# A decoder layer on one core: the correction pass of the attention scores made 128 rows high, GpSimd's start put behind the loads of x, and the last output block done in two halves

## The chip, the core and the metric

The kernel runs on one core of a Trainium2 chip. Its engines are TensorE (PE in the profile, with its weight loads in a row of their own, PEld), VectorE (DVE), ScalarE (ACT), GpSimd (POOL) and SyncE (SP), which issues transfers. The metric is the device time of one execution in microseconds (us), and a lower one is better.

## The reference

One decoder layer over 512 tokens of width 1024, all in float32. Eight heads do causal attention with a forget gate (a running sum of log gates is added to the logits), eight do causal attention over three dilated windows with a penalty by distance, and both are followed by an output projection. Then a PEER feed-forward picks 16 experts for each of 8 heads and each token out of 16384 and sums them.

```python
xn = rms_norm(h, norm1_g[layer])
proj = xn @ w_in[layer]
...
fox_out = fox_attention(fq, fk, fv, log_f)
dil_out = dilated_attention(dq, dk, dv)
mixed = jnp.concatenate([merge_heads(fox_out), merge_heads(dil_out)], axis=-1)
h = h + mixed @ w_out[layer]
xn2 = rms_norm(h, norm2_g[layer])
h = h + peer_ffn(xn2, peer_wq[layer], peer_subkeys[layer], peer_u[layer], peer_v[layer])
return rms_norm(h, normf_g)
```

## The kernel before, in words

Nearly every product is float32 done by splitting: a number is held as a high part (`hi`, rounded to the type that TensorE reads fast) and a low part (`lo`, what is left), and `mm3` (lines 147 to 153) sums three products hi·hi, hi·lo and lo·hi. ScalarE makes the high part, VectorE the low one.

**Start (lines 248 to 293).** SyncE issues the four blocks of x (128 tokens each), then the weights. ScalarE issues the unit matrix and two small vectors. GpSimd clears `cpart` and issues six loads of constants: `sel`, `maskb`, `iota16`, `mult`, `ndist`, `iota`. The sums of squares of x are taken by ScalarE (blocks 0 and 2, line 277) and by VectorE (blocks 1 and 3, line 278). `normed` (lines 126 to 145) turns a pair of sums into a scaled unit matrix `diag` and transposes x through TensorE with it; ScalarE (line 142) and VectorE (line 143) take the result out of PSUM. Only then do the projections begin, and from there on TensorE has work without a break.

**Attention (lines 323 to 436).** There are four groups `g` of four heads; groups 0 and 1 are the forget-gate heads, 2 and 3 the dilated ones. `project(g)` makes for each head the queries `qs` and keys `kT` as 128-row tiles: `kT` holds the high part of the key in its own 64 rows and the low part in the other 64, `qs` the high part of the query in both halves. `ql` holds the low part of the query, two heads in one tile, each in its 64 rows. `scores` (line 363) does for each head and each block of 128 queries

```python
own = slice(e * HD, (e + 1) * HD)
nc.tensor.matmul(s[:, :n], qs[:, h, i * P:n], kT[:, h, :n], start=True, stop=False)
nc.tensor.matmul(s[:, :n], ql[own, pr, i * P:n], kT[own, h, :n], start=False, stop=(g >= 2))
```

The first (line 373) contracts over 128 rows, the second (line 374, here called the correction pass) over 64. Both stream n = 128, 256, 384 or 512 columns. In groups 0 and 1 two short bfloat16 passes follow (lines 378 and 379: gate sums and mask). Then come the softmax on VectorE and ScalarE (lines 380 to 394), the transposes of the weights p on TensorE (`trans`, line 401), their copy by ScalarE (line 403) and the product with the values (line 424), of which each writes 64 of 128 rows. `attend` runs these as a pipeline of pairs of heads: 32 pairs in all, and a pair's transposes are issued one step after its scores. The score tile `s` in PSUM has 2 buffers, p has 5. `merge` interleaves `attend(g)` with `project(g + 1)`, and a scheduler then fixes the order of the instructions of each engine.

**The rest.** Output projection and second norm (lines 452 to 472), the choice of the experts (lines 556 to 725), and the dense stage (lines 757 to 797), in which each pair of 128 experts gets its products by lines 152 and 792. The tile `oacc[b][d]` sums the output of token block b and column half d. After the loop the last block's 24 matmuls, which alternate between the halves d = 0 and d = 1, end TensorE's work. The tail (lines 800 to 824) adds each block to the residual (line 810), sums squares (lines 812 and 814), and scales (line 821).

Of the kernel before, what the change touches and what calls it, by code (L numbers as in the profile page):

```python
# [71 lines left out]
def tile_kernel(ctx: ExitStack, tc: tile.TileContext, x, w_in, w_f, b_f, w_out, wq, skT, u, v, uT, g1, g2, g2r, gfr,  # L72
# [53 lines left out]
    def normed(pp, src, b0, ss, g, name, then=None):  # L126

        diag = small.tile([P, 2, P], F32, name="diag")
# [103 lines left out]
    with ExitStack() as st:  # L232
# [6 lines left out]
        mult = abf.tile([P, TB, P], F32, name="mult")  # L239
# [3 lines left out]
        qss = [qkv.tile([P, 4, T], F32R, name=f"qs{i}") for i in range(2)]  # L243
        qls = [qkv.tile([P, 2, T], F32R, name=f"ql{i}") for i in range(2)]
# [3 lines left out]
        with ExitStack() as s1:  # L248
# [18 lines left out]
            with tc.manual_schedule(engines={ET.Pool}):  # L267
                nc.gpsimd.memset(cpart, 0.0)
                for t, src in ((sel, csel), (maskb, cmask), (iota16, ciota16)):
                    nc.gpsimd.dma_start(t, src)  # L270
                nc.gpsimd.dma_start(mult, cmult)
                nc.gpsimd.dma_start(ndist, cdist)
                nc.gpsimd.dma_start(iota, ciota)
            nc.vector.tensor_copy(identb, ident)
            ss = small.tile([P, TB], F32, name="n1ss")
            for b0 in range(0, TB, 2):
                nc.scalar.activation(junk[0], xs[b0 // 2][:, 0, :], AF.Square, accum_out=ss[:, b0:b0 + 1])
                nc.vector.tensor_tensor_reduce(out=junk[1], in0=xs[b0 // 2][:, 1, :], in1=xs[b0 // 2][:, 1, :], scale=1.0, scalar=0.0,
                                               op0=ALU.mult, op1=ALU.add, accum_out=ss[:, b0 + 1:b0 + 2])
                _, _, norm1 = normed(xt, xs[b0 // 2], b0, ss[:, b0:b0 + 2], g1c, "n1", feed.start if b0 else None)  # L280
# [42 lines left out]
            def project(g):  # L323
                qs, ql, kT, vs = qss[g % 2], qls[g % 2], kTs[g % 2], vss[g % 2]
                for kind in range(3):
                    w = feed.get()
                    for n in range(2):
                        ps = pj.tile([P, T], F32, name="pj")
                        if kind < 2:
                            mm3(ps, cols(w, n), XT)  # L330
                            for e in range(2):
                                h = 2 * n + e
                                own, oth = slice(e * HD, (e + 1) * HD), slice((1 - e) * HD, (2 - e) * HD)
                                if kind == 0:
                                    sc = 1.0 / math.sqrt(HD) / (1.0 if g < 2 else SLOPES[4 * (g - 2) + h])
                                    hi = qs[own, h, :]
                                    nc.scalar.activation(hi, ps[own], AF.Copy, scale=sc)
                                    nc.scalar.activation(qs[oth, h, :], ps[own], AF.Copy, scale=sc)
# [24 lines left out]
        def scores(g, i, pr):  # L363
            qs, ql, kT = qss[g % 2], qls[g % 2], kTs[g % 2]
# [4 lines left out]
            for e in range(2):  # L369
                h = 2 * pr + e  # L370
                s = pS.tile([P, T], F32, name="s")
                own = slice(e * HD, (e + 1) * HD)
# [79 lines left out]
        for c in range(D // WC):  # L452
# [4 lines left out]
            for b in range(0, TB, 2):  # L457
# [9 lines left out]
                if c == D // WC - 1:  # L467
                    ss = small.tile([P, 2], F32, name="n2ss")
                    nc.vector.tensor_reduce(ss, sq[:, b:b + 2, :], axis=AX.X, op=ALU.add)
                    rs, norm2, _ = normed(xt, hb, b, ss, g2t, "n2")  # L470
# [256 lines left out]
    with ExitStack() as st:  # L727
# [29 lines left out]
        def dense():  # L757
            load_v(0)
            load_v(1)
            for i in range(NPAIR + 1):  # L760
# [18 lines left out]
                if i > 0:  # L779
# [5 lines left out]
                    for j, (n, c, b) in enumerate(order):  # L785
# [4 lines left out]
                        for w, m, s0, s1 in ((ah, vh, first_, False), (al, vh, False, False), (ah, vl, False, last_)):  # L790
                            for d in range(2):
# [108 lines left out]
```

## Time and profile before

| | |
|---|---|
| median of 3 runs | 1567.56 us (1567.28 to 1568.92) |
| the profiled execution | 1568.9 us |
| its span, first instruction to last | 1567.0 us |
| mean granted clock of TensorE | 0.992 of full |
| busy share of the span: TensorE, its weight loads, VectorE, ScalarE, GpSimd | 97%, 86%, 77%, 41%, 24% |
| chain that ended last: TensorE, VectorE, ScalarE, transfers | 82%, 12%, 3%, 2% |

The profiled execution is 1.3 us above the median, and 1.9 us of its time lie outside the span. Busy shares are of the whole span. Matmuls are pipelined: a matmul's own duration overlaps the next one's, so the distance from one start to the next says what a matmul costs. "Idle before" and the waits name the engine and the tile whose work ended last before an instruction could start; "issue" is time in which nothing that the profile shows was waited for. Where the heights of the two operands matter, the profile writes them before the shape: 64\*128 is a pass over 64 rows with 128 columns of weights.

### The profile page before, as it was taken

The numbers are of one execution on the slowest core, as the hardware profiler recorded it, in microseconds if no ns is written. First come the engines' busy times: TensorE is split into PE (matmuls) and PEld (weight loads), VectorE is DVE, ScalarE is ACT, GpSimd is POOL, SyncE is SP. The second block draws the span as 40 slices with busy tenths as digits, with TensorE's granted clock in tenths as the row PEclk, the third lists the DMA queues.
The fourth block names the chain that finished last, engine by engine and source line by source line (L and its number), as shares of the span: only waits on it lengthen the run. The fifth ranks groups of instructions, "written<-read, shape, count | busy, mean of one in ns | idle before, by whom it ended". The sixth has DMA issues, their size and how long they took to land.

```text
span 1567.0 us, 22166 instructions
## 1 busy us (share of the span) xinstructions
PE 1524.7 (97%) x8637; PEld 1344.4 (86%) x8641; DVE 1205.0 (77%) x2251; ACT 649.0 (41%) x804; POOL 377.9 (24%) x269
## 2 busy tenths in 40 slices
PE   6999999989999999999999999999999999999997
PEld 6777777978899898989888889888898888988886
DVE  6554476439999999996877787787778787877886
ACT  6354454332233766767333333333333333333332
POOL 1000000000002010001345435444444343444440
PEclk9999999999999999999999999999999999999999
DMA  5211110422237585868999898989999999998984
GB/s 198 82 54 55 55 54 29 175 81 81 82 138 265 219 296 198 303 225 326 373 365 349 327 325 316 364 312 338 331 324 333 328 338 325 324 322 324 345 273 161
DMA packets 139289, 380.39 MB, mean 243 GB/s; under 512 B 9392, under 2 KB 58672, under 8 KB 134448
## 3 DMA queue, kind: packets, MB, share of 16 engines
q1 hardware_dynamic: 95968, 228.87, 41.4%
q0 software_dynamic: 37600, 135.09, 23.3%
q10 hardware_dynamic: 5616, 15.02, 2.5%
q8 instruction: 68, 1.11, 0.3%
q14 instruction: 37, 0.30, 0.1%
HBM read 338.90 MB, written 40.37 MB: 242 GB/s over the span
## 4 chain that ended last, share of the span: by engine, by line
PE 82%; DVE 12%; ACT 3%; DMA 2%; issue 1%; SPq 0%; DVEq 0%; ACTq 0%
PE pj L152 39%; PE oa L792 33%; DVE wlo L124 3%; PE pg L711 2%; PE o L424 2%; PE s L374 1%; PE t L401 1%; PE xt L140 1%; ACT whi L123 1%; PE s L373 1%; ACT gs L701 1%; PE psc L576 1%; DVE og L689 1%; DMA gt<-Gd 1%; DVE eq L651 1%
## 5 line engine op out<-in xcount | busy, mean ns | idle before, releaser
L152 PE MATMUL pj<-xh,whi 128*128 128x384 f32 (+1 forms) x1288 | 453.0, 352 | 5.9 <-ACT hs L523 3.6
L152 PE MATMUL pj<-xh,wlo 128*128 128x384 f32 (+1 forms) x1288 | 451.7, 351 | 1.5 <-DVE wlo L124 1.5
L152 PE MATMUL pj<-xl,whi 128*128 128x384 f32 (+1 forms) x1288 | 450.1, 349 | 0.0
L493 POOL DMA_INDIRECT row<-in_u_dram,eidx x128 | 190.0, 1485 | 691.7 <-DVE hid L502 276.4
L123 ACT ACTIVATE whi<-wraw 128x2048 fp32r<-128x2048 f32 (+1 forms) x89 | 169.8, 1908 | 264.0 <-PE pj L152 254.8
L152 PEld LDWEIGHTS pj<-xh,whi 128*128 128x128 f32 x1288 | 243.4, 189 | 20.2 <-issue 4.7
L152 PEld LDWEIGHTS pj<-xh,wlo 128*128 128x128 f32 x1288 | 243.2, 189 | 12.6 <-DVE wlo L124 2.1
L152 PEld LDWEIGHTS pj<-xl,whi 128*128 128x128 f32 x1288 | 243.3, 189 | 11.2
L124 DVE TENSOR_TENSOR wlo<-wraw,whi 128x2048 fp32r<-128x2048 f32 (+1 forms) x89 | 202.3, 2274 | 55.6 <-ACT whi L123 55.6
L493 POOL DMA_INDIRECT row<-in_v_dram,eidx x128 | 182.2, 1423 | 242.3 <-DVE acc L509 211.3
L792 PE MATMUL oa<-vh,ah 128*128 128x512 f32 x768 | 237.3, 390 | 1.3 <-ACT ah L123 1.3
L792 PE MATMUL oa<-vh,al 128*128 128x512 f32 x768 | 237.5, 390 | 0.3 <-DVE al L124 0.3
L792 PE MATMUL oa<-vl,ah 128*128 128x512 f32 x768 | 237.6, 391 | 0.0
L123 ACT ACTIVATE vh<-vr 128x2048 fp32r<-128x2048 f32 x64 | 122.9, 1920 | 242.9 <-PE oa L792 213.3
L509 DVE SCALAR_TENSOR_TENSOR acc<-row,a,acc 128x1024 f32<-128x1024 f32 x128 | 164.2, 1283 | 20.9 <-DMA row<-in_v_dram,eidx 18.3
L792 PEld LDWEIGHTS oa<-vh,al 128*128 128x128 f32 x768 | 144.3, 188 | 31.3 <-DVE al L124 0.7
L792 PEld LDWEIGHTS oa<-vl,ah 128*128 128x128 f32 x768 | 144.6, 188 | 30.5
L502 DVE CUSTOM_DVE_ANT_0 row<-row,xn 128x1024 f32<-128x1024 f32 x128 | 152.1, 1220 | 22.3 <-DMA row<-in_u_dram,eidx 22.3
L792 PEld LDWEIGHTS oa<-vh,ah 128*128 128x128 f32 x768 | 143.9, 188 | 29.3 <-ACT ah L123 1.6
L124 DVE TENSOR_TENSOR vl<-vr,vh 128x2048 fp32r<-128x2048 f32 x64 | 146.2, 2285 | 0.0
L772 DVE TENSOR_TENSOR ga<-gt,ga 128x384 f32<-128x384 f32 x128 | 67.9, 553 | 65.4 <-ACT ga L523 57.4
L124 DVE TENSOR_TENSOR al<-ga,ah 128x768 fp32r<-128x768 f32 x64 | 61.3, 958 | 62.0 <-ACT ah L123 62.0
(207 smaller groups left out, 1639.7 us busy)
## 6 DMA issues: line engine op xcount, KB each, us to landing
wraw<-in_uT_dram SPq DMA_DIRECT2D x64, 1024.0 KB
vr<-in_v_dram SPq DMA_DIRECT2D x64, 1024.0 KB
Gd<-gs SPq DMA_DIRECT2D x12, 2048.0 KB
gt<-Gd SPq DMA_DIRECT2D x32, 768.0 KB
wraw<-in_w_in_dram SPq DMA_DIRECT2D x12, 1024.0 KB
Hd<-hs ACTq DMA_DIRECT2D x28, 384.0 KB
ga<-Hd SPq DMA_DIRECT2D x28, 384.0 KB
wraw<-in_wq_dram SPq DMA_DIRECT2D x8, 1024.0 KB
```

What stands on the lines that cost most here:

```text
L123: nc.scalar.activation(hi, src, AF.Copy)
L124: nc.vector.tensor_sub(lo, src, hi.bitcast(F32))
L140: nc.tensor.matmul(pt[:, kc % 2, e, :], src[:, e, kc * P:(kc + 1) * P], diag[:, e, :], start=True, stop=True)
L152: nc.tensor.matmul(ps, a, c, start=(i == 0), stop=(i == 3 * n - 1))
L373: nc.tensor.matmul(s[:, :n], qs[:, h, i * P:n], kT[:, h, :n], start=True, stop=False)
L424: nc.tensor.matmul(o[e * HD:(e + 1) * HD, pr, :], vs[:, j, h * HD:(h + 1) * HD], pts[e][:, j * P:(j + 1) * P], start=(j == 0), stop=(j == i))
L493: nc.gpsimd.indirect_dma_start(out=rows[n], out_offset=None, in_=tab, in_offset=bass.IndirectOffsetOnAxis(ap=eidx[:, k:k + 1], axis=0))
L502: nc.vector.tensor_tensor_reduce(out=t, in0=t, in1=xn0, scale=1.0, scalar=0.0, op0=ALU.mult, op1=ALU.add, accum_out=hid0[:, k:k + 1])
L509: nc.vector.scalar_tensor_tensor(acc, t, a0[:, k:k + 1], acc, op0=ALU.mult, op1=ALU.add)
L711: nc.tensor.matmul(pg[:, tt, :], w[2][:, t4 + tt, :], w[3][:, n, t4 + tt, :], start=(n == 0), stop=(n == 1))
L772: nc.vector.tensor_mul(a, gt[:, :, c, :], a)
L792: nc.tensor.matmul(oacc[b][d], w[:, c, sl], m[:, c, d * 512:(d + 1) * 512], start=s0, stop=s1)
```

## The change

There are three parts.

1. **Correction pass.** `ql` is gone. `qs` gets a second plane: `qs[:, 1, h, :]` holds the low part of the query in the head's own 64 rows, and zeros in the other 64. Both score passes now contract over 128 rows. To make room, `mult` becomes bfloat16, p has 4 buffers instead of 5, and `diag` moves into pools of the two norms, which end early. The zeros are written once, by four fills of GpSimd.
2. **GpSimd's start.** Its first fill waits for VectorE's sum of squares of the last block of x (line 270 of the new kernel), and with it the six loads of constants and the four new fills, which stand behind it.
3. **Last block.** The last block's 24 matmuls do all twelve of half d = 0 first, then all twelve of d = 1.

```diff
-    def normed(pp, src, b0, ss, g, name, then=None):
+    def normed(pp, sp, src, b0, ss, g, name, then=None):
-        diag = small.tile([P, 2, P], F32, name="diag")
+        diag = sp.tile([P, 2, P], F32, name="diag", bufs=2)
...
-        mult = abf.tile([P, TB, P], F32, name="mult")
+        mult = abf.tile([P, TB, P], BF16, name="mult")
-        qss = [qkv.tile([P, 4, T], F32R, name=f"qs{i}") for i in range(2)]
-        qls = [qkv.tile([P, 2, T], F32R, name=f"ql{i}") for i in range(2)]
+        qss = [qkv.tile([P, 2, 4, T], F32R, name=f"qs{i}") for i in range(2)]
...
-            with tc.manual_schedule(engines={ET.Pool}):
-                nc.gpsimd.memset(cpart, 0.0)
-                for t, src in ((sel, csel), (maskb, cmask), (iota16, ciota16)):
-                    nc.gpsimd.dma_start(t, src)
-                nc.gpsimd.dma_start(mult, cmult)
-                nc.gpsimd.dma_start(ndist, cdist)
-                nc.gpsimd.dma_start(iota, ciota)
...
+            with tc.manual_schedule(engines={ET.Pool}):
+                first = nc.gpsimd.memset(cpart, 0.0)
+                tc.add_manual_dep(first.ins, sums.ins.name, mybir.DependencyInfo(mybir.DependencyClass.Sync, mybir.DependencyReason.DATA),
+                                  reason="the loads of x come first")
+                for t, src in ((sel, csel), (maskb, cmask), (iota16, ciota16), (mult, cmult), (ndist, cdist), (iota, ciota)):
+                    nc.gpsimd.dma_start(t, src)
+                for i in range(2):
+                    z = qss[i][:, 1].rearrange("p (a b) t -> p a b t", b=2)
+                    nc.gpsimd.memset(z[0:HD, :, 1, :].bitcast(F32), 0.0)
+                    nc.gpsimd.memset(z[HD:P, :, 0, :].bitcast(F32), 0.0)
...
-                                    nc.vector.scalar_tensor_tensor(ql[own, n, :], ps[own], sc, hi.bitcast(F32), op0=ALU.mult, op1=ALU.subtract)
+                                    nc.vector.scalar_tensor_tensor(qs[own, 1, h, :], ps[own], sc, hi.bitcast(F32), op0=ALU.mult, op1=ALU.subtract)
...
-                nc.tensor.matmul(s[:, :n], qs[:, h, i * P:n], kT[:, h, :n], start=True, stop=False)
-                nc.tensor.matmul(s[:, :n], ql[own, pr, i * P:n], kT[own, h, :n], start=False, stop=(g >= 2))
+                for part in range(2):
+                    nc.tensor.matmul(s[:, :n], qs[:, part, h, i * P:n], kT[:, h, :n], start=(part == 0), stop=(part == 1 and g >= 2))
-                p = wk.tile([P, T], F32, name="p", bufs=5)
+                p = wk.tile([P, T], F32, name="p", bufs=4)
...
-                    for j, (n, c, b) in enumerate(order):
+                    halves = [(e, (0, 1)) for e in order if i < NPAIR or e[2] < TB - 2]
+                    halves += [(e, (d,)) for d in range(2) for e in order if i == NPAIR and e[2] == TB - 2]
+                    for j, ((n, c, b), ds) in enumerate(halves):
...
-                            for d in range(2):
+                            for d in ds:
```

GpSimd's queue from its first fill, before (names are tiles; `in_...` are inputs; the row's end is the shape):

```order
L268 MEMSET cpart 128x512
L270 DMA sel<-in_csel_dram 128x1024
L270 DMA maskb<-in_cmask_dram 128x128
L270 DMA iota_112<-in_ciota_dram 128x16
L271 DMA mult<-in_cmult_dram 128x512
L272 DMA ndist<-in_cdist_dram 128x512
L273 DMA iota<-in_ciota_dram 128x128
L308 MEMSET ln 128x512
L482 MEMSET acc 128x1024
```

The same queue in the changed kernel, in which the first of these rows waits for VectorE:

```order
L276 MEMSET cpart 128x512
L280 DMA sel<-in_csel_dram 128x1024
L280 DMA maskb<-in_cmask_dram 128x128
L280 DMA iota_112<-in_ciota_dram 128x16
L280 DMA mult<-in_cmult_dram 128x512
L280 DMA ndist<-in_cdist_dram 128x512
L280 DMA iota<-in_ciota_dram 128x128
L283 MEMSET qs_128 64x2x512
L284 MEMSET qs_128 64x2x512
L283 MEMSET qs_129 64x2x512
L284 MEMSET qs_129 64x2x512
L312 MEMSET ln 128x512
```

The six loads keep their order and stand behind the wait; the four fills of `qs` come after them and before the fill of `ln`, which the gates need.

VectorE's queue at the end of the program, before. `oa_7574` and `oa_7575` are the last block's halves d = 0 and d = 1, L810 adds them, L814 squares, L109 to L114 make the scale, and the L821 pair scales the block before the last:

```order
L810 TENSOR_TENSOR row<-row,oa_7574 128x512
L810 TENSOR_TENSOR row<-row,oa_7575 128x512
L109 RECIPROCAL n3r<-n3s 128x1
L814 ISA vh,n3ss<-row 128x512
L814 ISA n3ss 128x1
L111 SCALAR_TENSOR_TENSOR n3t<-n3r 128x1
L817 TENSOR_TENSOR n3sm<-n3ss 128x1
L112 TENSOR_TENSOR n3t<-n3t,n3v 128x1
L105 TENSOR_SCALAR n3v<-n3sm 128x1
L114 SCALAR_TENSOR_TENSOR n3q<-n3t,n3r 128x1
L821 SCALAR_TENSOR_TENSOR row<-row,n3q,vr 128x512 x2
L109 RECIPROCAL n3r<-n3s 128x1
```

The same place in the changed kernel; here the halves are `oa_7576` and `oa_7577`, and L816, L820, L823 and L827 stand for L810, L814, L817 and L821. First the five rows from the add of d = 0 on, in which the L827 pair scales the second block:

```order
L816 TENSOR_TENSOR row<-row,oa_7576 128x512
L114 SCALAR_TENSOR_TENSOR n3q<-n3t,n3r 128x1
L823 TENSOR_TENSOR n3sm<-n3ss 128x1
L827 SCALAR_TENSOR_TENSOR row<-row,n3q,vr 128x512 x2
L105 TENSOR_SCALAR n3v<-n3sm 128x1
```

and the rows right behind them, up to the pair that scales the block before the last:

```order
L816 TENSOR_TENSOR row<-row,oa_7577 128x512
L820 ISA vh,n3ss<-row 128x512
L820 ISA n3ss 128x1
L109 RECIPROCAL n3r<-n3s 128x1
L823 TENSOR_TENSOR n3sm<-n3ss 128x1
L111 SCALAR_TENSOR_TENSOR n3t<-n3r 128x1
L105 TENSOR_SCALAR n3v<-n3sm 128x1
L112 TENSOR_TENSOR n3t<-n3t,n3v 128x1
L114 SCALAR_TENSOR_TENSOR n3q<-n3t,n3r 128x1
L109 RECIPROCAL n3r<-n3s 128x1
L827 SCALAR_TENSOR_TENSOR row<-row,n3q,vr 128x512 x2
```

The add of d = 0 has moved up by five rows, and the first step of the last block's scale (the second L109) now stands ahead of the L827 pair, where it stood behind it. On TensorE, VectorE and ScalarE every other instruction stands where it stood, the attention included: a correction pass stands in each place where one stood.

## Rows read from the trace of the kernel before

**Rows 1.** The page, section 1: busy us, share, instructions of each engine.

```profile
PE 1524.7 (97%) x8637; PEld 1344.4 (86%) x8641; DVE 1205.0 (77%) x2251; ACT 649.0 (41%) x804; POOL 377.9 (24%) x269
```

**Rows 2.** Busy times of the attention's stretch: PE, PEld, DVE, ACT, POOL; clock, DMA.

```profile
57.00:275.00 218.00, 215.12 (x1368) 166.21 (x1371) 114.09 (x307) 106.18 (x230) 0.95 (x1) 0.99 0.15 54
```

**Rows 3.** Waits, 57 to 275 us: who <- what: us in total, times, longest.

```profile
PEld s L374 <- issue: 9.6, 42, 0.3
...
PEld L378 <- issue: 3.7, 17, 0.3
...
DVE p L384 <- PE t L401: 0.6, 1, 0.6
```

**Rows 4.** The correction pass by its line: duration ns min/median/max, first and last start.

```profile
L374 PE MATMUL s<-kT,ql x64: 322/410/503, 57.0 to 265.4; 64*128 64x128 f32 x16, 64*128 64x256 f32 x16, 64*128 64x384 f32 x16, 64*128 64x512 f32 x16
```

**Rows 5.** Timeline of TensorE, 256 columns: start us, us, instruction.

```profile
248.65 0.28 PE L373 MATMUL s<-kT,qs 128*128 128x256 f32 x1
248.86 0.38 PE L374 MATMUL s<-kT,ql 64*128 64x256 f32 x1
...
249.40 0.28 PE L152 MATMUL pj<-wlo,mixh 128*128 128x256 f32 x1
249.51 0.28 PE L373 MATMUL s<-kT,qs 128*128 128x256 f32 x1
```

**Rows 6.** The same view, 512 columns.

```profile
259.47 0.39 PE L373 MATMUL s<-kT,qs 128*128 128x512 f32 x1
...
260.44 0.28 PE L152 MATMUL pj<-wlo,mixh 128*128 128x256 f32 x1
```

**Rows 7.** The same view, 128 columns.

```profile
130.28 0.22 PE L373 MATMUL s<-kT,qs 128*128 128x128 f32 x1
...
130.68 0.23 PE L378 MATMUL s<-cpart,sel 128*128 128x128 bf16 x1
```

**Rows 8.** TensorE's timeline at its one long wait in the attention.

```profile
72.08 0.33 PE L373 MATMUL s<-kT,qs 128*128 128x128 f32 x1 [1.35 <-ACT p L381]
```

**Rows 9.** Timeline: last multiplication of p and first transpose behind it, first pair, last-but-one pair.

```profile
72.61 0.48 DVE L394 TENSOR_SCALAR p<-p,rz 128x128 f32<-128x128 f32 x2
...
73.30 0.39 PE L401 MATMUL t<-ident,p 128*128 128x128 f32 x2
...
267.94 0.88 DVE L394 TENSOR_SCALAR p<-p,rz 128x512 f32<-128x512 f32 x2
...
268.58 0.63 PE L401 MATMUL t<-ident,p 128*128 128x128 f32 x4
```

**Rows 10.** Busy times as in rows 2, after the wait of rows 8; clock 0.58.

```profile
73.00:77.00 4.00, 4.00 (x14) 3.16 (x15) 1.93 (x7) 1.74 (x7) 0.00 (x0) 0.58 0.01 4
```

**Rows 11.** VectorE's timeline at the start: first `diag`, last block of x.

```profile
8.47 0.42 DVE L131 TENSOR_TENSOR diag<-ident,n1q 128x256 f32<-128x256 f32 x1
10.89 1.22 DVE L278 CUSTOM_DVE_ANT_0 junk<-xs 128x1024 bf16<-128x1024 f32 x1 [1.99 <-DMA xs<-in_x_dram]
```

**Rows 12.** SyncE's DMA queue in 4 to 5 us, then 5 to 8 us: packets, MB, share.

```profile
q1 hardware_dynamic: 105, 0.41, 98.7%
...
q1 hardware_dynamic: 159, 0.57, 51.2%
```

**Rows 13.** Timeline: a fill of GpSimd beside a VectorE instruction with two inputs.

```profile
40.37 2.28 DVE L124 TENSOR_TENSOR wlo<-wraw,whi 128x2048 fp32r<-128x2048 f32 x1
...
40.58 0.53 POOL L308 MEMSET ln<- 128x512 f32 x1 [35.84 <-ACT qs L338]
```

**Rows 14.** The page, section 5: the same VectorE instruction in all its places.

```profile
L124 DVE TENSOR_TENSOR wlo<-wraw,whi 128x2048 fp32r<-128x2048 f32 (+1 forms) x89 | 202.3, 2274 | 55.6 <-ACT whi L123 55.6
```

**Rows 15.** VectorE's timeline in the tail.

```profile
1557.69 1.29 DVE L810 TENSOR_TENSOR row<-row,oa 128x512 f32<-128x512 f32 x2 [1.07 <-PE oa L792]
...
1560.27 1.41 DVE L821 SCALAR_TENSOR_TENSOR row<-row,n3q,vr 128x512 f32<-128x512 f32 x2
...
1562.38 0.75 DVE L821 SCALAR_TENSOR_TENSOR row<-row,n3q,vr 128x512 f32<-128x512 f32 x1
```

More of the change, by code (lines that the diff above doesn't have):

```diff
@@ L277, in tile_kernel @@
                 nc.scalar.activation(junk[0], xs[b0 // 2][:, 0, :], AF.Square, accum_out=ss[:, b0:b0 + 1])
-                nc.vector.tensor_tensor_reduce(out=junk[1], in0=xs[b0 // 2][:, 1, :], in1=xs[b0 // 2][:, 1, :], scale=1.0, scalar=0.0,
+                sums = nc.vector.tensor_tensor_reduce(out=junk[1], in0=xs[b0 // 2][:, 1, :], in1=xs[b0 // 2][:, 1, :], scale=1.0, scalar=0.0,
                                                op0=ALU.mult, op1=ALU.add, accum_out=ss[:, b0 + 1:b0 + 2])
-                _, _, norm1 = normed(xt, xs[b0 // 2], b0, ss[:, b0:b0 + 2], g1c, "n1", feed.start if b0 else None)
+                _, _, norm1 = normed(xt, xp, xs[b0 // 2], b0, ss[:, b0:b0 + 2], g1c, "n1", feed.start if b0 else None)
+            with tc.manual_schedule(engines={ET.Pool}):
[8 more added lines that the diff above has]
+                    nc.gpsimd.memset(z[HD:P, :, 0, :].bitcast(F32), 0.0)
             pf = pj.tile([P, T], F32, name="pj")
@@ L323, in project @@
             def project(g):
-                qs, ql, kT, vs = qss[g % 2], qls[g % 2], kTs[g % 2], vss[g % 2]
+                qs, kT, vs = qss[g % 2], kTs[g % 2], vss[g % 2]
                 for kind in range(3):
@@ L335, in project @@
                                     sc = 1.0 / math.sqrt(HD) / (1.0 if g < 2 else SLOPES[4 * (g - 2) + h])
-                                    hi = qs[own, h, :]
+                                    hi = qs[own, 0, h, :]
                                     nc.scalar.activation(hi, ps[own], AF.Copy, scale=sc)
-                                    nc.scalar.activation(qs[oth, h, :], ps[own], AF.Copy, scale=sc)
-                                    nc.vector.scalar_tensor_tensor(ql[own, n, :], ps[own], sc, hi.bitcast(F32), op0=ALU.mult, op1=ALU.subtract)
+                                    nc.scalar.activation(qs[oth, 0, h, :], ps[own], AF.Copy, scale=sc)
+                                    nc.vector.scalar_tensor_tensor(qs[own, 1, h, :], ps[own], sc, hi.bitcast(F32), op0=ALU.mult, op1=ALU.subtract)
                                 else:
@@ L363, in scores @@
         def scores(g, i, pr):
-            qs, ql, kT = qss[g % 2], qls[g % 2], kTs[g % 2]
+            qs, kT = qss[g % 2], kTs[g % 2]
             n = (i + 1) * P
@@ L469, in tile_kernel @@
                     nc.vector.tensor_reduce(ss, sq[:, b:b + 2, :], axis=AX.X, op=ALU.add)
-                    rs, norm2, _ = normed(xt, hb, b, ss, g2t, "n2")
+                    rs, norm2, _ = normed(xt, hp, hb, b, ss, g2t, "n2")
                     if b == 0:
```

1 line of the change is left out of this document (removed).

## The prediction

> **What bounds the kernel now.** I read the page first: TensorE is busy 1524.7 us, 97% of the span, VectorE 77% [rows 1]. A busy share of pipelined matmuls need not mean that the engine is well used, so I went by stretches. The attention runs from 57 to 275 us, and there TensorE is busy 215.1 of 218 us, VectorE 114.1, ScalarE 106.2 [rows 2]. So TensorE sets the pace and the softmax engines have room on average; what a pair of heads needs at one moment is another question, below. The waits of that stretch show something odd: TensorE's weight loader stands 9.6 us ahead of the correction pass L374 and 3.7 us ahead of L378, which follows it, and both are "issue", waiting for no other engine [rows 3].
>
> **Part 1, the correction pass: what one costs.** There are 64, 16 of each width [rows 4]. I take start to next start. At 256 columns, four matmuls (L373, L374 and two L152) go from 248.65 to 249.51, 0.86 us; a full-height neighbour of that width gives way to the next after 0.11 [rows 5]; I take 0.115, so four of them should take 0.46. The half-height pass costs 0.40 us too much: some of it before it, some behind it, until full-height matmuls run again at their own distance. At 512 columns L373, L374 and an L152 of 256 go from 259.47 to 260.44, 0.97 us [rows 6]; by twice the distance of 256 columns for the wide ones that should be 0.23 + 0.23 + 0.115, so 0.39 too much. At 128 columns L373 and L374 take from 130.28 to 130.68, 0.40 us [rows 7]; at 0.115 each, 0.17 too much. For 384, between its neighbours, I take 0.39. Sum: 16 x (0.17 + 0.40 + 0.39 + 0.39) = 21.6 us. Some passes stand just ahead of L424, whose weights are 64 columns wide and which may cost a change of its own, so I take 20. The lower bound is the idle time of the weight loader alone, 9.6 + 3.7 = 13.3 [rows 3]; the upper is 21.6.
>
> The changed pass has 128 rows and the same columns, so I price it as a full-height pass. The Trainium skill's page "TensorE: Matmul & The Clock Gate" (Part 2, step by step) speaks against a gain here: a matmul's distance to the next follows from its columns, and the number of rows doesn't matter. By that alone a 64-row pass costs what a 128-row pass costs, and part 1 would bring nothing. The rows disagree, 0.86 against 0.46. The page "TensorEngine Tiling (Array Packing)" (Key Properties) has the rule that fits them: another tiling mode drains the engine first.
>
> **What of it comes back as waits.** The order on the engines is unchanged in the attention, so TensorE comes to each place that needs the softmax earlier, while the softmax takes as long as before. One such place has no room already: the score pass at 72.08 waits 1.35 us for an exponential [rows 8]. For the others I compared, for all 32 pairs, the end of the multiplication of p with the start of its transposes. Eight pairs have under 0.5 us of room; the first ends at 73.09 and is used at 73.30, the last has one head's half done at about 268.4 and is used at 268.58 [rows 9]. Between a pair's scores and its transposes lie two to three other correction passes, so TensorE would be there 0.8 to 1.1 us sooner than now, against 0.1 to 0.5 us of room. I lose 0.6 us in each of the eight, about **5 us**; what is lost at one place is room at the next, so it does not add up further. Bounds: 0, if the softmax starts sooner by as much as TensorE arrives sooner, and 8 x 1.1 = 9.
>
> With 4 buffers for p instead of 5, the first softmax instruction of a head (L384) waits for the transposes of the head four before, not five. With 5 that wait is seen once, 0.6 us [rows 3]. I count it among the 5 us; its bounds are 0 and one such wait for each of the last group's 8 pairs, 5 us. `mult` in bfloat16 and the moved `diag` change no instruction count, and VectorE is idle 104 of these 218 us [rows 2]: nothing. Part 1 gives 20 - 5 = **15 us**.
>
> **Part 2, the start.** TensorE waits for x. VectorE's sum of squares of the last block starts at 10.89, when its load has landed, having idled 1.99 us behind the first `diag`, which ends at 8.89 [rows 11]. SyncE's queue moved 0.41 MB in the microsecond 4 to 5, but 0.57 MB in the three from 5 to 8 [rows 12], when the constants came in. At the first rate it would have moved 1.23, so 0.66 MB, or 1.6 us, were given to the constants. With GpSimd waiting, x lands 1.6 us sooner at least, and the same competition up to the landing should give more; VectorE is free from 8.89, so no more than 2.0 helps. What follows (second `diag`, 16 results taken from PSUM by ScalarE and VectorE, first projection) is one chain of compute and shifts as a whole. I take **2.0 us**; bounds 1 and 2.4.
>
> Behind GpSimd's new wait stand the six loads, the four fills and the fill of `ln`. The loads' first reader is the score stage, from 57 us on [rows 4]. A fill of 512 columns took 0.53 us, while VectorE's instruction beside it took 2.28 us [rows 13], as others of its kind do on average (2.274 us [rows 14]). Four fills of 1024 columns are at most 8 x 0.53 = 4.2 us, ended by about 20 us, ahead of `ln` at 40.58: nothing. If such a fill held VectorE up, the price would be up to 4.2 us, as VectorE sets the start at that time.
>
> **Part 3, the last block.** VectorE adds both halves from 1557.69 on, 1.29 us together [rows 15]. With d = 0 done twelve matmuls sooner, only the second add, 0.64, is left when TensorE ends, and its input is there one matmul, some 0.23, later than 1557.69. So 0.4 us are saved so far. But by the order, nine rows of short instructions and then the pair that scales the block before the last (1.41 us, from 1560.27 [rows 15]) still stand between it and the end. The first reciprocal of the last block's scale now comes ahead of that pair and has to wait for ScalarE's root. So half of the 0.4 us is taken as used up there: **0.2 us**, bounds 0 and 0.64.
>
> **Sum.** 15 + 2.0 + 0.2 = 17.2 us off the profiled execution, 1568.9, gives 1551.7. That execution is 1.3 above the median of the runs, 1567.56, from which the same sum gives **1550.4 us**.
>
> **The rivals.**
>
> *All of it counts.* Nothing comes back: 20 + 2.2 off the median, 1545.4. For it: VectorE's and ScalarE's free time [rows 2], and a softmax that starts sooner since its scores do. Against: the eight narrow places, and one with no room at all [rows 8, 9].
>
> *The softmax takes over.* The gain is the lower bound, 13.3, and 5 us come back: 8.3 + 2.2 off, 1557.1. For it: in the last group no projection is left to fill the gaps, and the lost buffer of p bites there.
>
> *The height costs nothing.* If a pass costs what its columns cost, the 0.40 us belongs to the score tiles, and only the start and tail remain, 1567.6 - 2.2 = 1565.4, within the 0.2%. Against it: L373 has the same score tile and the same width, and from one before it takes its place after the usual 0.11 [rows 5].
>
> *Slower: the clock falls again and again.* After the wait of 1.35 us TensorE was granted 0.58 of its clock from 73 to 77 us [rows 8, 10], that is, mostly 1.2 instead of 2.4 GHz, and lost 0.42 x 4 = 1.7 us. If the time taken from the correction passes turns into such a wait in each of the 32 pairs, 32 x 1.7 = 54 us are lost, 37 more than is won: 1604. It decides from eleven such drops on (17.2 / 1.7). The skill's page "TensorE: Matmul & The Clock Gate" (Part 1) has this mechanism: the clock follows how busy the engine has been, and gaps halve it. Against it: the stretch's mean clock is 0.99 [rows 2], so it happened once, and the new waits would be half as long as that one.
>
> **How the numbers follow.** Forecast 62%, all counts 15%, softmax takes over 15%, height costs nothing 4%, clock 4%. 0.2%, or 3.1 us, is about what a measurement of this kernel can tell from no change. The first three are faster by more: 92%; the fourth is the same: 4%; the fifth slower: 4%. The range goes from the upper bounds of the gross gain with little lost, 1567.6 - (21.6 + 2.4 + 0.6) = 1543, rounded in to 1544.5, to the softmax case, 1558; outside lie the last two and the edges of the first three, under 2 in 10.
>
> **What would show it.** Right: the weight loader's "issue" wait in front of the second score pass is gone, two score passes of 256 columns follow each other at about 0.12 us, the first long run of L152 starts some 2 us sooner, and TensorE has new waits of 0.2 to 1 us for VectorE and ScalarE in the attention, about 5 us in all. The end of the last matmul to the end of the span stays as long as it is, to 0.5 us. Wrong: the second pass still shows a distance of 0.2 us or more; x lands at 10 us or later although GpSimd waits; the granted clock falls in the attention more than two or three times.

## The result and the profile after

The changed kernel takes **1551.95 us** (median of 4 runs, 1551.69 to 1552.48); the kernel before, run beside it, 1567.42. The ratio is 0.9899, with a 95% interval of 0.9887 to 0.9911: 1.0% faster. The forecast was 1550.4, its range 1544.5 to 1558. The profiled execution after took 1551.99 us with a span of 1550.2, so 16.8 us of span are gone against the one before (1567.0).

The page of the kernel after, its span and its section 1; [rows 1] is the same line before:

```profile
span 1550.2 us, 22175 instructions
...
PE 1507.3 (97%) x8637; PEld 1339.7 (86%) x8641; DVE 1204.7 (78%) x2251; ACT 649.7 (42%) x804; POOL 381.8 (25%) x273
```

TensorE has the same 8637 instructions and 17.4 us less to be busy with; GpSimd has its four fills more. Where the 16.8 us lie was read from one landmark to the next:

| from ... to | before | after | gained |
|---|---|---|---|
| span's start ... first unbroken run of L152 | 21.35 | 19.85 | 1.50 |
| ... last transpose of p (L401, now L404) starts | 251.52 | 237.16 | 14.36 |
| ... last matmul starts | 1284.62 | 1284.06 | 0.56 |
| ... span's end | 9.56 | 9.16 | 0.40 |

**Start.** VectorE's timeline after; [rows 11] answer to it:

```profile
8.51 0.42 DVE L131 TENSOR_TENSOR diag<-ident,n1q 128x256 f32<-128x256 f32 x1
9.72 1.23 DVE L270 CUSTOM_DVE_ANT_0 junk<-xs 128x1024 bf16<-128x1024 f32 x1 [0.80 <-DMA xs<-in_x_dram]
...
12.78 0.43 DVE L131 TENSOR_TENSOR diag<-ident,n1q 128x256 f32<-128x256 f32 x1
```

The last block of x is there 1.17 us sooner, and VectorE still waits 0.80 us for it. SyncE's queue in 4 to 5 us, and then in 5 to 8 us (packets, MB, share), as in [rows 12]:

```profile
q1 hardware_dynamic: 106, 0.41, 98.8%
...
q1 hardware_dynamic: 271, 0.97, 86.3%
```

It moved 0.97 MB in the three us in place of 0.57, not the 1.23 that the forecast took. GpSimd's timeline after:

```profile
11.02 0.53 POOL L276 MEMSET cpart<- 128x512 bf16 x1 [10.56 <-DVE n1ss L270]
...
14.83 1.03 POOL L283 MEMSET qs<- 64x1024 f32 x1
```

The wait holds GpSimd until 11.02, and the fills end at 18.85, ahead of the attention.

**Attention.** TensorE's timeline after, 128, 256 and 512 columns; "x2" is two passes that follow each other, and the second row of a group is the instruction up to whose start the group is counted:

```profile
125.15 0.33 PE L377 MATMUL s<-kT,qs 128*128 128x128 f32 x2
125.33 0.23 PE L381 MATMUL s<-cpart,sel 128*128 128x128 bf16 x1
...
235.52 0.40 PE L377 MATMUL s<-kT,qs 128*128 128x256 f32 x2
...
236.00 0.40 PE L377 MATMUL s<-kT,qs 128*128 128x256 f32 x2
...
244.34 0.63 PE L377 MATMUL s<-kT,qs 128*128 128x512 f32 x2
...
244.93 0.27 PE L152 MATMUL pj<-wlo,mixh 128*128 128x256 f32 x1
```

These are the places of [rows 5 to 7]. At 128 columns the two score passes that took 0.40 us take 125.33 - 125.15 = 0.18. The four matmuls that took 0.86 us take 236.00 - 235.52 = 0.48, and the three that took 0.97 take 244.93 - 244.34 = 0.59. The waits of TensorE for exponentials before, 53 to 278 us, and then the waits after, 53 to 262 us, first of TensorE and then of its weight loader (who <- what: us in total, times, longest):

```profile
PE s L373 <- ACT p L381: 1.3, 1, 1.3
```

```profile
PE s L377 <- ACT p L384: 2.3, 3, 1.6
PE t L404 <- DVE p L397: 1.0, 2, 0.5
```

```profile
PEld s L377 <- ACT p L384: 3.8, 4, 2.0
PEld L381 <- issue: 3.7, 17, 0.3
PEld o L427 <- ACT pt L406: 3.1, 10, 0.5
...
PEld s L377 <- issue: 0.7, 4, 0.2
```

The loader's 9.6 us of "issue" ahead of the correction pass [rows 3] are 0.7 us, over both score passes. The 3.7 us in 17 places ahead of the next line (L378 before, L381 now) are still there, to the tenth. And the new waits have come, for exponentials and for p. The longest is that of [rows 8]; here it is in TensorE's timeline:

```profile
70.56 0.44 PE L377 MATMUL s<-kT,qs 128*128 128x128 f32 x2 [1.59 <-ACT p L384]
```

and the busy times behind it, as in [rows 10] (the last three figures: granted clock, DMA share, GB/s):

```profile
72.00:76.00 4.00, 4.00 (x13) 3.13 (x12) 1.34 (x4) 1.23 (x7) 0.00 (x0) 0.60 0.02 4
```

**Tail.** VectorE's timeline after; [rows 15] answer to it:

```profile
1538.77 0.69 DVE L816 TENSOR_TENSOR row<-row,oa 128x512 f32<-128x512 f32 x1 [0.49 <-PE oa L798]
...
1541.49 0.69 DVE L816 TENSOR_TENSOR row<-row,oa 128x512 f32<-128x512 f32 x1 [0.45 <-PE oa L798]
...
1543.56 0.16 DVE L109 RECIPROCAL n3r<-n3s 128x1 f32<-128x1 f32 x1
...
1545.53 1.41 DVE L827 SCALAR_TENSOR_TENSOR row<-row,n3q,vr 128x512 f32<-128x512 f32 x2
```

The add of d = 0 is done 2.7 us ahead of the add of d = 1, and the second reciprocal (L109) waits for nothing. The last L827 pair starts 1545.53 - 1541.07 = 4.46 us behind the start of the last matmul, where the L821 pair started 4.89 behind it before.

**Between.** The 0.56 us arise at one place. Windows of the kernel before and of the kernel after (clock third from the end):

```profile
749.00:753.00 4.00, 3.96 (x10) 3.12 (x11) 4.00 (x2) 1.91 (x1) 0.00 (x0) 0.57 1.09 347
```

```profile
730.00:737.00 7.00, 6.52 (x29) 4.94 (x28) 6.09 (x5) 2.87 (x3) 0.00 (x0) 1.00 1.06 370
```

The profiled execution before had one fall of the clock more, at the entry of the dense stage, behind a wait of 1.25 us for `ah` (748.05). From 720 to 753 us it fell 2.6 us further behind the one after, and by 768 us it had 2.0 of them back, as the kernel after waited for `ah` a little later (1.0 and 0.4 us). That belongs to the execution rather than to the change: two executions below without part 1 (parts 2 and 3 alone) don't have it there either.

### The profile page after: what moved, and what is told of

Read it like the earlier page. It is cut to its first block, busy times and chain, and to the rows that moved or that the text cites. A ratio compares the mean times of both kernels' runs of the same rounds, so it can differ in the third digit from the quotient of the medians.

```text
span 1550.2 us, 22175 instructions
## 1 busy us (share of the span) xinstructions
PE 1507.3 (97%) x8637; PEld 1339.7 (86%) x8641; DVE 1204.7 (78%) x2251; ACT 649.7 (42%) x804; POOL 381.8 (25%) x273
## 4 chain that ended last, share of the span: by engine, by line
PE 79%; DVE 13%; ACT 3%; DMA 2%; issue 2%; SPq 0%; DVEq 0%; ACTq 0%
PE pj L152 39%; PE oa L798 33%; DVE wlo L124 3%; PE pg L714 2%; PE o L427 2%; PE s L377 1%; PE xt L140 1%; PE t L404 1%; ACT whi L123 1%; ACT gs L704 1%; PE psc L579 1%; DVE og L692 1%; DMA vr<-in_v_dram 1%; DVE eq L654 1%; DVE eq L651 1%
## 5 line engine op out<-in xcount | busy, mean ns | idle before, releaser
L152 PE MATMUL pj<-xh,whi 128*128 128x384 f32 (+1 forms) x1288 | 453.1, 352 | 5.6 <-ACT hs L526 3.3
L152 PE MATMUL pj<-xh,wlo 128*128 128x384 f32 (+1 forms) x1288 | 451.6, 351 | 1.5 <-DVE wlo L124 1.5
L152 PE MATMUL pj<-xl,whi 128*128 128x384 f32 (+1 forms) x1288 | 450.2, 350 | 0.0
L152 PEld LDWEIGHTS pj<-xh,whi 128*128 128x128 f32 x1288 | 243.5, 189 | 19.9 <-issue 4.7
L152 PEld LDWEIGHTS pj<-xh,wlo 128*128 128x128 f32 x1288 | 243.5, 189 | 12.4 <-DVE wlo L124 2.1
L152 PEld LDWEIGHTS pj<-xl,whi 128*128 128x128 f32 x1288 | 243.7, 189 | 10.9
L124 DVE TENSOR_TENSOR wlo<-wraw,whi 128x2048 fp32r<-128x2048 f32 (+1 forms) x89 | 202.4, 2274 | 57.2 <-ACT whi L123 57.2
L124 DVE TENSOR_TENSOR vl<-vr,vh 128x2048 fp32r<-128x2048 f32 x64 | 146.2, 2285 | 0.0
L124 DVE TENSOR_TENSOR al<-ga,ah 128x768 fp32r<-128x768 f32 x64 | 61.3, 958 | 61.3 <-ACT ah L123 61.3
```

The lines of the kernel that those rows point to most:

```text
L124: nc.vector.tensor_sub(lo, src, hi.bitcast(F32))
L152: nc.tensor.matmul(ps, a, c, start=(i == 0), stop=(i == 3 * n - 1))
```

## The experiments

### Each part alone

Part 1 alone is the diff without the wait and without the halves; GpSimd clears its tiles and loads from the start on, and fills `qs` at once. Part 2 alone and part 3 alone are their diff lines on the kernel before:

```diff
+                first = nc.gpsimd.memset(cpart, 0.0)
+                tc.add_manual_dep(first.ins, sums.ins.name, ...)
```

```diff
+                    halves = [(e, (0, 1)) for e in order if i < NPAIR or e[2] < TB - 2]
+                    halves += [(e, (d,)) for d in range(2) for e in order if i == NPAIR and e[2] == TB - 2]
```

> The kernel before with part 1 alone (128-row correction pass, zeros, 4 buffers of p); GpSimd's start and the last block as before. Theory: the change between 128 and 64 rows costs about 0.4 us a pass, 20 us in all, and some 5 us come back as waits for the softmax. Of the 15.5 us that the whole change took off, part 1 should have 14 to 14.5, so 1553.2 us +- 0.7; the last transpose of the attention should stand 14.3 us earlier than before. Rival, the start did it (what TensorE loses at the start multiplies through the merged order): 1566 us. Rival, the fills of zeros in the middle of the start hold VectorE up: first long run of L152 up to 4 us later than before.

> The kernel before with part 2 alone: GpSimd's fill and its six loads of constants wait for VectorE's sum of the last block of x. Theory: the constants took bandwidth from x; x lands 1.2 us sooner and the unbroken run of L152 starts 1.5 us sooner (19.85 instead of 21.35 us), as in the changed kernel; 1565.9 us +- 0.5. Rival, the wait of GpSimd costs the attention's start (gate sums or masks late): no gain, 1567.4, with a wait of the first score passes longer than 1.35 us.

> The kernel before with part 3 alone: the last block's twelve matmuls of the left half first. Theory: from the start of the last matmul to the end of the span 9.56 us become 9.13 as in the changed kernel, so 0.4 us less, 1567.0 us, which the runs can hardly tell from 1567.4. Rival, matmuls that follow each other into one half are slower than alternating ones: 24 matmuls take longer than 5.45 us.

| part | median us | ratio to before, 95% interval |
|---|---|---|
| 1, the pass | 1554.3 | 0.9911 (0.9896 to 0.9926) |
| 2, the start | 1566.77 | 0.9991 (0.9982 to 1.0) |
| 3, the halves | 1567.19 | 0.9997 (0.9988 to 1.0006) |

The kernel before took 1568.49 us beside these runs, 1.07 more than the 1567.42 from which the expected times were worked out, so the times of parts 1 and 2 lie above their expected ranges, and the ratios are what to read: 14.0 us off for part 1, where 14 to 14.5 were expected. The three ratios add up to -1.01%, the whole's -1.01%; the parts don't visibly disturb each other, though the intervals leave room for some 0.2%. Part 1 carries it, and its last transpose stands 14.3 us earlier, as expected. The 24 matmuls of the last block take 5.21 us from first to last start before and with part 3 alone, so its rival falls. Parts 2 and 3 by themselves are below what the comparison tells from no change; only their profiles show them: the tail's 9.56 us became 9.12 with part 3 alone, and the long run of L152 started at 20.32 with part 2 alone.

Part 1's attention took 235.63 us between the landmarks of the table, 1.5 less than the whole change's. The reason is the clock, and it shows which way a wait can go. TensorE's timeline in part 1 alone, and the busy times behind the wait:

```profile
73.68 0.44 PE L378 MATMUL s<-kT,qs 128*128 128x128 f32 x2 [1.59 <-ACT p L385]
```

```profile
74.00:78.00 4.00, 4.00 (x24) 3.30 (x23) 2.39 (x9) 2.33 (x8) 0.00 (x0) 1.00 0.01 4
```

The wait is the same, 1.59 us, and here the granted clock stayed full. With the fall the stretch is 1.5 us longer. The kernel before has it both ways too: 251.52 us with the fall, 249.94 in part 3 alone, without. So like is compared with like: with the fall, 251.52 - 237.16 = 14.4; without it, 249.94 - 235.63 = 14.3.

### Is it the buffer of p? (4 before, 5 after)

```diff
-                p = wk.tile([P, T], F32, name="p", bufs=5)
+                p = wk.tile([P, T], F32, name="p", bufs=4)
```

> The kernel before with 4 instead of 5 buffers for p and nothing else. Theory: where a softmax instruction has to wait for transposes of the head four before, it waits under a microsecond, in the last group alone, and TensorE has other work there: 1567.4 to 1568.0 us. Rival, the lost buffer is what takes 5 us of the gain back: 1572 us.

The kernel before with 4 buffers: 1568.97 us, ratio 1.0005 (0.9996 to 1.0014). The time is above the expected 1568.0, but so is the kernel before beside it (1568.49). The attention took 249.88 us between the landmarks, against 249.94 in part 3 alone, both without a fall of the clock. The other way round, the changed kernel with 5; room is made by putting the small vectors `z`, `rz` and `m` into one tile:

> The changed kernel with 5 buffers of p again (the small softmax vectors share one tile, to make room). Theory: the lost buffer costs under 1 us; the order in the last group changes: 1551.0 to 1552.2 us. Rival (the lost buffer causes most of the waits that came back): 1548 us.

It took 1552.2 us, ratio 0.9903 (0.9888 to 0.9918), as the changed kernel does, and TensorE is idle for 5.07 us in the attention, as against 5.06. The buffer is not where the waits come from.

### What makes the 64-row pass dear?

Two experiments on the kernel before. The first nearly halves the number of changes of height (70 in place of 128, counted in the traces): both heads' high passes first, then both correction passes.

```diff
+            for e in range(2):
+                high = nc.tensor.matmul(ss_[e][:, :n], qs[:, 2 * pr + e, i * P:n], kT[:, 2 * pr + e, :n], start=True, stop=False)
...
+                with behind(high):
+                    low = nc.tensor.matmul(ss_[e][:, :n], ql[own, pr, i * P:n], kT[own, 2 * pr + e, :n], start=False, stop=(g >= 2))
```

> The kernel before, with the two heads of a pair ordered as high pass, high pass, correction pass, correction pass: the same 64-row passes, half as many changes of height. Theory (the change of height is what costs): of about 20 us half goes, less what comes back as waits (both heads' scores are ready together, so the softmax of the first starts later): 6 to 10 us off, 1558 to 1561 us; start to next start from the first to the second correction pass of 256 columns about 0.12 us. Rival (a pass of 64 rows is slow in itself): no gain, 1567 us or more, and 0.3 us between the two.

1559.51 us, ratio 0.9943 (0.9929 to 0.9956): 0.57% or 8.9 us off, inside the theory's 6 to 10. But the two correction passes don't follow each other at the expected 0.12 us. TensorE's timeline of this kernel:

```profile
254.28 0.49 PE L371 MATMUL s<-kT,qs 128*128 128x512 f32 x1
254.71 0.50 PE L375 MATMUL s<-kT,ql 64*128 64x512 f32 x2
255.14 0.87 PE L429 MATMUL o<-pt,vs 128*64 128x128 f32 x10
```

Two correction passes of 512 columns take 0.50 us together, and one L371 alone takes 0.49: they start 3 ns apart (3 or 4 in 29 of the 32 pairs) and run at the same time, the heads' rows being different halves. That is what the Trainium skill's page "TensorE: Matmul & The Clock Gate" (Part 3, packing small matmuls) says of tiles in different rows of the array, and the trace agrees. So a part of the 8.9 us is a pass that runs beside another: its columns, by the full-height distances some 8 x (0.06 + 0.12 + 0.18 + 0.23) = 4.7 us in all, as an estimate. So this run doesn't separate the theory from the rival: two passes that are slow in themselves would gain by running at the same time too. The next experiment does. Even so the attention was longer than with full-height passes and zeros (241.70 us against 237.16, with one fall of the clock in each).

The second doubles the correction pass (its low part is added twice):

```diff
+                nc.tensor.matmul(s[:, :n], ql[own, pr, i * P:n], kT[own, h, :n], start=False, stop=False)
                 nc.tensor.matmul(s[:, :n], ql[own, pr, i * P:n], kT[own, h, :n], start=False, stop=(g >= 2))
```

> The kernel before with every correction pass done twice in a row (the low part of the query counts double, so the output changes). Theory (the change of height costs, not the height): the second one costs its columns alone, 16 x (0.06 + 0.12 + 0.175 + 0.23) = 9.4 us of TensorE time, at most 11 with the weight loads of the narrow ones: 1576 to 1579 us. Rival (the height itself costs 0.4 us a pass): 64 x (0.15 + 0.34) = 31 us more, 1598 us.

1584.09 us (1581.46 to 1586.13), ratio 1.0106 (1.009 to 1.0121). That is 1.06% or 16.6 us more, between the theory and the rival, so the trace has to tell. The attention is 11.25 us longer (262.77 against 251.52, each with one fall of the clock), close to the theory's 9.4 to 11 and far from the rival's 31; 2.4 more lie around it in the profiled execution, and the last 3 are between that execution and the medians and are not located. TensorE and then its weight loader in this kernel:

```profile
255.16 0.28 PE L373 MATMUL s<-kT,qs 128*128 128x256 f32 x1
255.37 0.38 PE L374 MATMUL s<-kT,ql 64*128 64x256 f32 x1
255.59 0.28 PE L375 MATMUL s<-kT,ql 64*128 64x256 f32 x1
255.80 0.39 PE L373 MATMUL s<-kT,qs 128*128 128x256 f32 x1
```

```profile
255.05 0.19 PEld L373 LDWEIGHTS s<-kT,qs 128*128 128x128 f32 x1
255.37 0.18 PEld L374 LDWEIGHTS s<-kT,ql 64*128 64x128 f32 x1
255.48 0.19 PEld L375 LDWEIGHTS s<-kT,ql 64*128 64x128 f32 x1
255.80 0.19 PEld L373 LDWEIGHTS s<-kT,qs 128*128 128x128 f32 x1
```

Read the loads against their matmuls. Where the height stays (128 to 128 at 255.05, 64 to 64 at 255.48), a load starts 0.11 us ahead of its matmul, beside the matmul before. Where it changes, up or down, load and matmul start together (255.37 and 255.80), 0.21 us behind the start of the pass before, which is 0.09 more than that pass's usual distance. It looks as if the load waits for the pass before to run out; as the ends are modelled (255.44 for the one before 255.37), the trace doesn't show what exactly it waits for. The first pass of the new height then lasts 0.38 or 0.39 us, 0.1 longer than the 0.28 of one whose load was ahead. So a change costs some 0.1 us ahead of it and 0.1 for a load in plain view; a correction pass makes two changes, 0.4. The second 64-row pass makes none, and adds 0.22 + 0.21 - 0.31 = 0.12 us (the last number is from L374 to the next in [rows 5] and the row behind them, 248.86 to 249.17), its columns. Five of the 64 stood elsewhere in the order and made changes of their own, which is about the rest of the 11.25.

The rows of the loader before show the same at the same place:

```profile
248.54 0.19 PEld L373 LDWEIGHTS s<-kT,qs 128*128 128x128 f32 x1
248.86 0.18 PEld L374 LDWEIGHTS s<-kT,ql 64*128 64x128 f32 x1
249.17 0.19 PEld L152 LDWEIGHTS pj<-whi,mixh 128*128 128x128 f32 x1
```

### Would more work fill the new waits?

The changed kernel with its correction pass made twice (the low part is added twice):

```diff
-                for part in range(2):
-                    nc.tensor.matmul(s[:, :n], qs[:, part, h, i * P:n], kT[:, h, :n], start=(part == 0), stop=(part == 1 and g >= 2))
+                for j in range(3):
+                    nc.tensor.matmul(s[:, :n], qs[:, min(j, 1), h, i * P:n], kT[:, h, :n], start=(j == 0), stop=(j == 2 and g >= 2))
```

> The changed kernel with its 128-row correction pass done twice in a row (the low part of the query counts double, so the output changes). This adds 9.4 to 11 us of TensorE work in the attention. Theory (some 5 us of the gain came back as waits for the softmax): part of the added work fills those waits, so the time grows by less, 5 to 8 us, 1557 to 1560 us. Rival (TensorE waits for nothing, each microsecond counts in full): 10 to 11 us, 1562 to 1563 us.

1562.93 us (1560.83 to 1565.76), ratio 0.9965 (0.9952 to 0.9979), which is 0.66% or 10.3 us above the changed kernel's. The theory fell. The attention is 9.24 us longer (246.40), which is the columns of 64 passes at the full-height distances: 16 x (0.06 + 0.12 + 0.18 + 0.23) = 9.4. TensorE's waits in this kernel:

```profile
PE s L377 <- ACT p L384: 2.8, 3, 1.9
PE s L377 <- DVE m L387: 1.2, 2, 0.7
PE t L404 <- DVE p L397: 0.5, 1, 0.5
```

They did not get less (TensorE's idle time is 5.21 us, 5.06 in the changed kernel). The waits are no free room on TensorE. The reading that fits is that an exponential can only start behind the score passes of its own tile, and work put into those passes moves the exponential by as much as it moves TensorE.

### What else holds x up?

With GpSimd's loads gone the queue still did not keep its first rate. The changed kernel with ScalarE's load of `b_f` (512 bytes, issued beside x's loads) behind the last eviction of the normed x:

```diff
-            nc.scalar.dma_start(bft, b_f)
...
+            with behind(*norm1):
+                nc.scalar.dma_start(bft, b_f)
```

> The changed kernel, with ScalarE's load of b_f, which is issued beside x's loads, put behind the last eviction of the normed x. In the changed kernel the queue of x's loads moved 0.97 MB in the three us from 5 to 8, against 0.41 MB in the one us from 4 to 5, so something still slowed it although GpSimd's loads were gone. Theory: the small packets of b_f share the DMA engines with x; without them x's last block sum starts 0.1 to 0.5 us sooner than 9.72 and the time falls by as much, under 0.03%, which a comparison cannot tell from no change but the profile can. Rival: the queue's rate is its own, x's last sum stays at 9.6 to 9.9. Either way 1551.5 to 1552.5, ratio to the kernel before 0.988 to 0.991.

1551.63 us, ratio 0.9893 (0.9876 to 0.9909): nothing that can be told from the changed kernel. Its profile, though, answers the question: SyncE's queue and the small one of ScalarE in 5 to 8 us, then VectorE and TensorE:

```profile
q1 hardware_dynamic: 351, 1.25, 101.9%
q10 hardware_dynamic: 81, 0.00, 1.5%
```

```profile
8.87 1.22 DVE L269 CUSTOM_DVE_ANT_0 junk<-xs 128x1024 bf16<-128x1024 f32 x1
...
10.77 0.48 DVE L143 SCALAR_TENSOR_TENSOR xl<-xt,g1c,xh 128x256 fp32r<-128x256 f32 x1 [0.68 <-ACT xh L142]
...
12.80 0.42 DVE L131 TENSOR_TENSOR diag<-ident,n1q 128x256 f32<-128x256 f32 x1
```

```profile
19.89 0.47 PE L152 MATMUL pj<-xh,wlo 128*128 128x512 f32 x1
```

ScalarE's small queue had 222 packets in that time in the changed kernel and has 81 now. Half a kilobyte in such packets had slowed x's queue from 1.25 to 0.97 MB in these three us; in the three other kernels with part 2 and this load in its old place, the queue moved 0.85, 0.87 and 0.95. The Trainium skill's page "DMA: Bandwidth & Descriptors" (Specifications) asks for 512 bytes or more per transfer for the full rate. These packets are far below it; but that sentence is about the small transfer's own rate, and the loss of the load beside it is what these traces add. Now VectorE doesn't wait for x, whose sum starts at 8.87, 0.85 us sooner and not the 0.1 to 0.5 expected, and yet the second `diag` starts at 12.80, as before, and the long run at 19.89. VectorE's queue stands in the way: its scale chain for the second half (from L105 on) is behind the first results of the first half, which wait for ScalarE. The start is a compute chain from there on, and loading x sooner is worth nothing more here.

## Why the prediction was right, point by point

**Which part pays, and how much.** Part 1 was to give 15 us, part 2 2.0 and part 3 0.2. Measured: 14.4, 1.50 and 0.40, and 0.56 from another place, at a fall of the clock, that no part gave. The sum of 17.2 against 16.8 is closer than its terms, since their misses cancel. So do those inside part 1's term: 20 - 5 stands against 17.9 - 3.5, as follows. The mechanism was right; that the number is this close is in part luck.

**What a correction pass costs.** Laid side by side, the 1600 matmuls of both traces up to the end of the attention stand in the same order, so each distance can be compared. From the first unbroken run of L152 on, 6.6 us were saved into the correction pass, 10.3 out of it and 1.0 one further on, 17.9 in all; all other distances together lost 3.5. Distances that grew at the passes themselves come to 0.6, so 18.5 were gained there before these. The 20 was 1.5 to 2 us too high, since the forecast read its prices off dear places. There 0.38 were gained at 256 and at 512 columns, for 0.40 and 0.39. The median of all sixteen passes of a width was 0.23 at 128 columns (0.17 forecast) and 0.29 at 256, 384 and 512. In 27 of the 64 the next pass is L378, whose own load waits anyway, and there the median is 0.28; where it is L152, as in two of the forecast's three places, 0.36. The mechanism that decided between the Trainium skill's two rules in the prediction (columns alone, or a drained engine at each other tiling), that a change of height is paid going in and coming out, is shown by the load rows of the doubled pass.

**The lower bound was built on a wrong row.** It added the loader's 3.7 us ahead of L378 to the 9.6 ahead of L374. The 3.7 are still there. L378 is a bfloat16 pass behind a float32 one, and now follows a full-height pass, so that wait was never the height's. The 13.3 didn't enter the forecast, only the third case (softmax takes over, 1557.1) and with it the range's upper end.

**What came back.** 5 us were to return at eight narrow places. By the same comparison 3.5 returned net, and 5.0 is the sum of all distances that grew. Nine of these grew by more than 0.15 us, 3.1 together. Four are transposes that wait for p (184.21, 185.37, 218.19, 252.72), 1.6 us in three of the forecast's eight pairs. Four are score passes that wait for the softmax of the tile before (an exponential at 70.56, 127.08 and 129.03, a maximum at 233.43), 1.4 us; of these the forecast had named the first alone. So the kind of wait was right, and the places were right in part. Idle time shows less than half of it: TensorE's grew from 2.88 to 5.06 us; the rest is in weight loads that wait, such as the 3.1 us ahead of L427 (1.5 before). That the loss at one place is room at the next fits the sum, but wasn't tested; that 5.0 is the forecast's number is luck, at a flat 0.6 for each place.

**The buffer of p** cost nothing, in either direction; counting it among the 5 was harmless. The rival that leaned on it falls.

**The start: 2.0 forecast, 1.50 in the profile.** Two steps failed. x did not land 1.6 us sooner, but 1.17, since a second disturber, the packets of `b_f`, stayed; "at the first rate it would have moved 1.23" was true only without both. And "what follows shifts as a whole" was not so: the second `diag` moved by 0.89 us (13.67 to 12.78), and the long run by 1.50. Before, TensorE stood 1.12 us (up to 12.58) in the middle of the first half's transposes, for a result of VectorE (L143) that stood behind the sum of x. After, it doesn't wait there, and its transposes of the second half begin at 14.17 in place of 15.67, which is the 1.50. Single starts also scatter: without part 2 the long run began between 21.35 and 22.93 in six kernels, with it between 19.22 and 20.32 in five. The means of the two groups lie 2.5 us apart (22.3 and 19.8), so the 1.50 of one pair of executions is not the measure of the part; the runs with part 2 alone put it at 1.4 us, with 0 to 2.8 in the interval.

**The fills.** The four of `qs` cost nothing in the changed kernel: they ran from 14.83 to 18.85 beside L124 and L143, which took as long as before (L124 1.22 us in both). But [rows 13] doesn't hold for every instruction of VectorE, as these rows show. The first two are VectorE in part 1 alone, where fills ran from 4.65 to 5.67 and from 6.72 to 7.67; the other two are VectorE and GpSimd in the changed kernel:

```profile
4.78 0.97 DVE L277 CAST identb<-ident 128x128 bf16<-128x128 f32 x1 [3.90 <-DMA ident<-in_cident_dram]
...
7.28 0.42 DVE L105 TENSOR_SCALAR n1v<-n1ss 128x2 f32<-128x2 f32 x1
```

```profile
216.39 1.66 DVE L397 TENSOR_SCALAR p<-p,rz 128x512 f32<-128x512 f32 x2
```

```profile
216.70 1.06 POOL L485 MEMSET acc<- 128x1024 f32 x1 [177.08 <-PE s L377]
```

In the kernel before the same cast took 0.23 us and the same L105 0.17, and such a pair of multiplications 0.88 [rows 9]. Each of them (of the pair, the second multiplication) began beside a running fill and ended only after it. So one of the new waits, that of the transposes at 218.19, stands at a place that the fill of `acc` makes narrow, and it does so in the kernel before too (1.70 us for the pair, from 228.43). Putting that fill elsewhere wasn't tested.

**The tail: 0.2 forecast, 0.40 measured.** The half that was written off, because the second reciprocal would wait for ScalarE's root, was not lost: the root was ready 0.03 us before it was needed.

**The clock.** No new fall: the attention has one in the profiled execution before and one in the one after, behind the same wait. The rival that needed eleven had none more, though the waits grew.

## What to carry to other kernels

In these traces a weight load was not hidden behind the matmul before where the height changed. Other changes do the same: in the changed kernel the loads of 27 bfloat16 passes (L381) right behind a float32 pass, and of 33 passes of L152 right behind one with 64 columns of weights (L427), start within 5 ns of their matmul. So look for loads that start together with their matmul, and price each change by the extra distance on both sides, over many places and not a few, and not by the "issue" row that stands nearest. A half-height pass that changes the height twice can cost more than a full one padded with zeros. When a busy engine gets faster, it meets new waits in its own dependency chain. They can be estimated beforehand by comparing the ends of the producers with the starts of the readers, and here more work did not fill them.

## What the runs showed that was not expected

- Two 64-row passes on different halves of the rows started 3 ns apart and took the time of one (0.50 us at 512 columns).
- A load of 512 bytes slowed the loads beside it by a fifth or more for three us (0.85 to 0.97 MB in four traces, 1.25 without it).
- The same wait of 1.59 us was followed by a granted clock of 0.60 in one execution and of 1.00 in another; the fall costs 1.5 us here.
- A full-height load on the same 128 rows starts 0.11 us ahead of its matmul, beside the pass before of 256 columns (255.05 against 255.16).
- A cast and tensor-scalar instructions of VectorE that began beside a fill of GpSimd ended only after the fill (0.97 us in place of 0.23, and 1.66 in place of 0.88 for a pair), while those with two tensor inputs beside a fill took their usual time (1.22 us).
